# Group softmax over 285 MB: stores moved to GpSimdE's DMA queue, larger tiles, and another order at both ends

## The chip, the cores and the metric

The kernel runs on one core of a Trainium2 chip. Its data lie in the chip's memory (HBM) and pass through the core's on-chip buffer (SBUF, 128 partitions) by way of 16 DMA engines. Three compute engines matter: VectorE (DVE in the profile), ScalarE (ACT) and GpSimdE (POOL). SyncE (SP) computes nothing and issues DMAs. The engines run side by side and wait for one another on semaphores; a DMA adds 16 to its semaphore in all, one for each DMA engine that has finished its share.

The metric is the device time of one execution in microseconds (us): 1330.17 us before the change, the median of nine runs from 1329.59 to 1332.29.

## What is computed

```python
B, N, D, G = 4, 4096, 4352, 8
def reference(x):                      # x: (B, N, D) float32
    Dg = D // G                        # 544
    x_g = x.reshape(B, N, G, Dg)
    x_g = x_g - x_g.max(axis=-1, keepdims=True)
    exp = np.exp(x_g)
    out = exp / exp.sum(axis=-1, keepdims=True)
    return out.reshape(B, N, D)
```

Each of the 16,384 rows has eight groups of 544 numbers, and each group goes through a softmax of its own. Input and output are 285.2 MB each, and each is moved once: 570.4 MB.

## The kernel before

The rows are cut into 64 tiles. A tile is 256 rows of the matrix; each of the 128 partitions holds R = 2 whole rows of it, one after the other, which lie together in HBM too: 34,816 bytes. One such row on all 128 partitions (128 x 4352 elements, 2.2 MB) is the unit of computation, called a row below; there are 128 of them, numbered n, in ring slots s. The ring has NT = 5 buffers (line 50), and everything is done in place in them.

For each row there are four steps. `vector_max` (line 62) takes the maximum of the eight groups, negated, in one VectorE instruction. `scalar_exp` (line 79) lets ScalarE take the exponential of each group in turn, with the negated maximum as bias, and has it add up each group's sum on the way (eight instructions). `vector_scale` (line 68) takes the reciprocal of the eight sums and multiplies the row by it, two VectorE instructions.

The order on VectorE is written out (lines 130 to 143): the maximum of row n+1 stands before the scaling of row n, so that ScalarE has work while VectorE scales. The maximum of a tile's first row waits until the whole tile has landed (line 65), and so the scaling of a tile's last row, which stands behind it, waits for the next tile as well.

SyncE issues every DMA, both ways, on its one queue. It first loads four tiles (lines 107 and 108). After that, for each tile t, it waits until both of its rows are scaled and stores it (`store`, line 98), then waits until store t-1 has landed and loads tile t+4 into the buffer that this has freed (`step`, line 102). The loop runs twelve times over five steps, the rest is written out behind it, and at the end SyncE waits for the last five stores (lines 118 and 119). GpSimdE has nothing to do.

Of the kernel before, what the change touches and what calls it, by code (L numbers as in the profile page):

```python
# [1 line left out]

# [4 lines left out]


@with_exitstack
def kernel(  # L10
    ctx: ExitStack,
    tc: tile.TileContext,
    x: bass.AP,
    out: bass.AP,
):
    nc = tc.nc
    G = 8
    P = 128
    R = 2
    NT = 5  # L20
    S = R * NT
    AHEAD = NT - 1
    xf = x.flatten_outer_dims()
    of = out.flatten_outer_dims()
    N, D = xf.shape
    Dg = D // G
    nt = N // (P * R)
    nr = nt * R
    turns = (nr - 1) // S
    ring_turns = (nt - AHEAD) // NT  # L30
    steps = ring_turns * NT
    f32 = mybir.dt.float32
    X = mybir.AxisListType.X
    Exp = mybir.ActivationFunctionType.Exp
    xt = xf.rearrange("(t p r) d -> t p (r d)", p=P, r=R)
    ot = of.rearrange("(t p r) d -> t p (r d)", p=P, r=R)
    turn_in = xf[AHEAD * P * R:(AHEAD + steps) * P * R, :].rearrange(
        "(u b p r) d -> u b p (r d)", b=NT, p=P, r=R)
    turn_out = of[:steps * P * R, :].rearrange("(u b p r) d -> u b p (r d)", b=NT, p=P, r=R)

    landed = [tc.alloc_semaphore(f"landed{b}") for b in range(NT)]
    stored = [tc.alloc_semaphore(f"stored{b}") for b in range(NT)]

    max_done = tc.alloc_semaphore("max_done")
    exp_done = tc.alloc_semaphore("exp_done")
    rec_done = tc.alloc_semaphore("rec_done")
    scaled = tc.alloc_semaphore("scaled")

    ctx.enter_context(tc.tile_critical(no_gpsimd_drain=True))  # L49
    bufs = [ctx.enter_context(nc.sbuf_tensor(f"xt{b}", [P, R * D], f32)) for b in range(NT)]  # L50
    mx = ctx.enter_context(nc.sbuf_tensor("mx", [P, S, G], f32))
    sm = ctx.enter_context(nc.sbuf_tensor("sm", [P, S, G], f32))
    rs = ctx.enter_context(nc.sbuf_tensor("rs", [P, S, G], f32))

    def take(engine, sem, n=1):
        engine.sem_inc(sem, -n).wait_op(sem, n, "sem-ge")

    def row(s):
        b, r = divmod(s, R)
        return bufs[b][:, r * D:(r + 1) * D].rearrange("p (g d) -> p g d", g=G)  # L60

    def vector_max(s):
        i = nc.vector.reduce_max(out=mx[:, s, :], in_=row(s), axis=X, negate=True)  # L63
        if s % R == 0:
            i.wait_op(landed[s // R], 16, "sem-ge")
        i.then_inc(max_done, 1)

    def vector_scale(s):
        nc.vector.reciprocal(out=rs[:, s, :], in_=sm[:, s, :]).wait_op(  # L69
            exp_done, s + 1, "sem-ge").then_inc(rec_done, 1)  # L70
        xr = row(s)
        nc.vector.tensor_tensor(  # L72
            out=xr,
            in0=xr,
            in1=rs[:, s, :].unsqueeze(2).to_broadcast([P, G, Dg]),
            op=mybir.AluOpType.mult,
        ).wait_op(rec_done, s + 1, "sem-ge").then_inc(scaled, 1)

    def scalar_exp(s):
        xr = row(s)  # L80
        for g in range(G):
            i = nc.scalar.activation(  # L82
                out=xr[:, g, :],
                in_=xr[:, g, :],
                func=Exp,
                bias=mx[:, s, g:g + 1],
                scale=1.0,
                accum_out=sm[:, s, g:g + 1],
            )
            if g == 0:  # L90
                i.wait_op(max_done, s + 1, "sem-ge")
        i.then_inc(exp_done, 1)


    def load(t, source):
        nc.sync.dma_start(out=bufs[t % NT][:, :], in_=source).then_inc(landed[t % NT], 16)  # L96

    def store(t, target):
        take(nc.sync, scaled, R)
        nc.sync.dma_start(out=target, in_=bufs[t % NT][:, :]).then_inc(stored[t % NT], 16)  # L100

    def step(t, source, target):
        store(t, target)
        take(nc.sync, stored[(t - 1) % NT], 16)
        load(t + AHEAD, source)

    for t in range(AHEAD):
        load(t, xt[t])
    nc.sync.sem_inc(stored[NT - 1], 16)
    with nc.sync.Fori(0, ring_turns) as u:  # L110
        for t in range(NT):
            step(t, turn_in[u, t], turn_out[u, t])
    for t in range(steps, nt):
        if t + AHEAD < nt:
            step(t, xt[t + AHEAD], ot[t])
        else:
            store(t, ot[t])
    for t in range(nt - NT, nt):
        nc.sync.wait_ge(stored[t % NT], 16)

    nc.scalar.preload_act_table(Exp)  # L121
    with nc.scalar.Fori(0, turns):
        for s in range(S):
            scalar_exp(s)
        nc.scalar.sem_inc(max_done, -S)
    for n in range(turns * S, nr):
        scalar_exp(n % S)


    vector_max(0)  # L130
    with nc.vector.Fori(0, turns):
        for s in range(S):
            if s == S - 1:
                for b in range(NT):
                    nc.vector.sem_inc(landed[b], -16)
            vector_max((s + 1) % S)
            vector_scale(s)
        nc.vector.sem_inc(exp_done, -S)
        nc.vector.sem_inc(rec_done, -S)
    for n in range(turns * S, nr):  # L140
        if n + 1 < nr:
            vector_max((n + 1) % S)
        vector_scale(n % S)


# [1 line left out]
_INS = ['x']  # L147
_OUTS = [((4, 4096, 4352), 'float32')]


# [23 lines left out]
```

## Time and profile before

| | |
|---|---|
| median of nine runs | 1330.17 us |
| the profiled execution | 1331.32 us |
| its span in the profile | 1329.3 us |
| maximum of a row (VectorE, line 63), 128 times | 4681 ns |
| reciprocal of a row's sums (VectorE, line 69), 128 times | 193 ns |
| scaling of a row (VectorE, line 72), 128 times | 4692 ns |
| exponentials of a row (ScalarE, line 82, eight instructions) | 5.97 us |
| ScalarE's waiting for maxima, in all | 541.7 us |
| issue of a DMA on SyncE | 0.34 to 0.35 us |
| a load, from its issue to its landing (median of 64) | 30.6 us |
| a store, from its issue to its landing (median of 64) | 40.3 us |

The span is the part of the execution that the profile covers, and the execution is a little longer. The table's rows are durations of single instructions or transfers; whether they count depends on what they lie beside. A landing time holds the time that a transfer stands in the queue behind others, so it is no measure of how fast the transfer itself moves.

### The profile page before, as it was taken

The numbers are of one execution on the slowest core, as the hardware profiler recorded it, in microseconds if no ns is written. First come the engines' busy times: TensorE is split into PE (matmuls) and PEld (weight loads), VectorE is DVE, ScalarE is ACT, GpSimd is POOL, SyncE is SP. The second block draws the span as 40 slices with busy tenths as digits, with TensorE's granted clock in tenths as the row PEclk, the third lists the DMA queues.
The fourth block names the chain that finished last, engine by engine and source line by source line (L and its number), as shares of the span: only waits on it lengthen the run. The fifth ranks groups of instructions, "written<-read, shape, count | busy, mean of one in ns | idle before, by whom it ended". The sixth has DMA issues, their size and how long they took to land. (4 is left out here: it accounts for less than half of the span.)

```text
span 1329.3 us, 3155 instructions
## 1 busy us (share of the span) xinstructions
DVE 1207.8 (91%) x384; ACT 764.4 (58%) x2049; POOL 0.2 (0%) x4
## 2 busy tenths in 40 slices
DVE  5999999989898898998989989989899898998994
ACT  3656565655565555655556556555565555655652
POOL 0000000000000000000000000000000000000000
DMA  9999999999999999999999999999999999999997
GB/s 402 418 434 433 432 425 430 433 434 431 435 433 427 433 436 434 436 435 433 428 432 436 435 436 434 431 431 433 436 434 435 436 428 430 435 435 436 434 435 328
DMA packets 18435, 570.46 MB, mean 429 GB/s; under 512 B 2048, under 2 KB 2048, under 8 KB 2048
## 3 DMA queue, kind: packets, MB, share of 16 engines
q1 hardware_dynamic: 18432, 570.43, 99.6%
q14 instruction: 3, 0.02, 0.0%
HBM read 285.21 MB, written 285.21 MB: 429 GB/s over the span
## 5 line engine op out<-in xcount | busy, mean ns | idle before, releaser
L82 ACT ACTIVATE xt<-xt,mx 128x544 f32<-128x544 f32 x1024 | 751.3, 734 | 541.7 <-DVE mx L63 541.7
L63 DVE TENSOR_REDUCE mx<-xt 128x8 f32<-128x4352 f32 x128 | 599.1, 4681 | 97.2 <-DMA xt<-in_x_dram 97.2
L72 DVE TENSOR_TENSOR xt<-xt,rs 128x4352 f32<-128x4352 f32 x128 | 600.6, 4692 | 4.4
L82 ACT ACTIVATION_READ_ACCUMULATOR xt<-xt,mx 128x1 f32 x1024 | 191.0, 187 | 0.0
L69 DVE RECIPROCAL rs<-sm 128x8 f32<-128x8 f32 x128 | 24.7, 193 | 2.6 <-ACT xt L82 2.6
L121 ACT ACT_TABLE_LOAD x1 | 1.3, 1283 | 0.9 <-SPq L49 0.9
L158 POOL MEMSET const-bfloat16-1.0<- 128x1 bf16 x1 | 0.1, 101 | 0.0
L158 POOL MEMSET const-uint8-127<- 128x1 uint8 x1 | 0.1, 101 | 0.0
L158 POOL MEMSET const-float32-0.0<- 128x1 f32 x1 | 0.1, 98 | 0.2 <-issue 0.2
L158 POOL MEMSET const-float32-1.0<- 128x1 f32 x1 | 0.1, 98 | 0.0
## 6 DMA issues: line engine op xcount, KB each, us to landing
xt<-in_x_dram SPq DMA_DIRECT2D x64, 4352.0 KB, 30.6
out_dram<-xt SPq DMA_DIRECT2D x64, 4352.0 KB, 40.3
```

Of the source, the lines that this page charges most:

```text
L63: i = nc.vector.reduce_max(out=mx[:, s, :], in_=row(s), axis=X, negate=True)
L69: nc.vector.reciprocal(out=rs[:, s, :], in_=sm[:, s, :]).wait_op(exp_done, s + 1, "sem-ge").then_inc(rec_done, 1)
L72: nc.vector.tensor_tensor(out=xr, in0=xr, in1=rs[:, s, :].unsqueeze(2).to_broadcast([P, G, Dg]), op=mybir.AluOpType.mult,).wait_op(rec_don ...
L82: i = nc.scalar.activation(out=xr[:, g, :], in_=xr[:, g, :], func=Exp, bias=mx[:, s, g:g + 1], scale=1.0, accum_out=sm[:, s, g:g + 1],)
L121: nc.scalar.preload_act_table(Exp)
L158: nc = _bacc.Bacc("TRN2", target_bir_lowering=False, num_devices=1)
```

## The change

The ring has four buffers of three rows each (R = 3, NT = 4), so a partition's share of a tile is 52,224 bytes. There are 42 tiles of three rows and one of two.

SyncE issues all loads, written out one by one without a loop. Load t waits for store t-4 and for nothing else. The first and the last tile are loaded row by row, three and two DMAs, each row with a semaphore of its own, on which VectorE's maximum of that row waits.

GpSimdE issues the stores of tiles 0 to 40, each when its three rows are scaled. The stores of the last two tiles are issued by SyncE, behind its last load; they have their own semaphores, `last_scaled` and `last_stored`. GpSimdE waits for its last two stores and then runs a drain of its own, while SyncE's two are under way.

ScalarE's loop is built by another call, with an option that fixes where its first instruction stands; one more instruction ahead of the loop comes with it. What VectorE and ScalarE compute, and in which order, is as before.

```diff
-    R = 2
-    NT = 5
+    R = 3
+    NT = 4
...
+    sizes = nr // R * [R]
+    if nr % R:
+        sizes.append(nr % R)
+    nt = len(sizes)
     turns = (nr - 1) // S
-    ring_turns = (nt - AHEAD) // NT
+    LAST = 2
+    ring_turns = (nt - LAST) // NT
...
+    def tile_of(af, t):
+        lo = t * P * R
+        return af[lo:lo + P * sizes[t], :].rearrange("(p r) d -> p (r d)", p=P)
...
-    def vector_max(s):
+    def vector_max(n):
+        s = n % S
         i = nc.vector.reduce_max(out=mx[:, s, :], in_=row(s), axis=X, negate=True)
-        if s % R == 0:
+        r = n % R
+        if r == 0:
             i.wait_op(landed[s // R], 16, "sem-ge")
+        elif n < R:
+            i.wait_op(first_landed[r - 1], 16, "sem-ge")
+        elif n // R == nt - 1:
+            i.wait_op(last_landed[r - 1], 16, "sem-ge")
         i.then_inc(max_done, 1)
...
-        ).wait_op(rec_done, s + 1, "sem-ge").then_inc(scaled, 1)
+        ).wait_op(rec_done, s + 1, "sem-ge").then_inc(
+            scaled if n // R < nt - LAST else last_scaled, 1)
...
+    for t in range(nt):
+        if t >= NT:
+            nc.sync.wait_ge(stored[t % NT], 16 * (t // NT))
+        tile_in, source = bufs[t % NT], tile_of(xf, t)
+        if 0 < t < nt - 1:
+            nc.sync.dma_start(out=tile_in[:, :], in_=source).then_inc(landed[t % NT], 16)
+            continue
+        others = last_landed if t else first_landed
+        for r in range(sizes[t]):
+            nc.sync.dma_start(
+                out=tile_in[:, r * D:(r + 1) * D], in_=source[:, r * D:(r + 1) * D],
+            ).then_inc(others[r - 1] if r else landed[t % NT], 16)
+    rows = 0
+    for t in range(nt - LAST, nt):
+        rows += sizes[t]
+        nc.sync.wait_ge(last_scaled, rows)
+        nc.sync.dma_start(
+            out=tile_of(of, t), in_=bufs[t % NT][:, :sizes[t] * D]).then_inc(last_stored, 16)
+    nc.sync.wait_ge(last_stored, 16 * LAST)
...
     def store(t, target):
-        take(nc.sync, scaled, R)
-        nc.sync.dma_start(out=target, in_=bufs[t % NT][:, :]).then_inc(stored[t % NT], 16)
...
+        take(nc.gpsimd, scaled, R)
+        nc.gpsimd.dma_start(out=target, in_=bufs[t % NT][:, :]).then_inc(stored[t % NT], 16)
+
+    with nc.gpsimd.Fori(0, ring_turns) as u:
         for t in range(NT):
-            step(t, turn_in[u, t], turn_out[u, t])
...
+            store(t, turn_out[u, t])
+    for t in range(steps, nt - LAST):
+        store(t, tile_of(of, t))
+    for t in range(nt - NT, nt - LAST):
+        nc.gpsimd.wait_ge(stored[t % NT], 16 * (t // NT + 1))
+    nc.gpsimd.drain()
 
     nc.scalar.preload_act_table(Exp)
-    with nc.scalar.Fori(0, turns):
+    with nc.Fori(0, turns, engines=OrderedEngineSet([nc.scalar.engine]),
+                 head_slot={nc.scalar.engine: 0}):
         for s in range(S):
             scalar_exp(s)
```

## The prediction

> **What bounds the kernel now.** I read the busy rows first, then the queue table, then the loads and stores of the last third in order of time, the stretches, and last the chain of waits. From the page:
>
> ```profile
> DVE 1207.8 (91%) x384; ACT 764.4 (58%) x2049; POOL 0.2 (0%) x4
> ...
> q1 hardware_dynamic: 18432, 570.43, 99.6%
> ...
> HBM read 285.21 MB, written 285.21 MB: 429 GB/s over the span
> ```
>
> The 16 DMA engines are busy all the time; VectorE has 121 us of slack, ScalarE more. So time is bytes over rate, plus what is lost at the ends. The issues of SyncE, in order of time (start, duration):
>
> ```profile
> 1194.02 0.34 SPq L96 DMA_DIRECT2D xt<-in_x_dram  x1
> 1194.61 0.35 SPq L100 DMA_DIRECT2D out_dram<-xt  x1
> 1214.59 0.34 SPq L96 DMA_DIRECT2D xt<-in_x_dram  x1
> 1215.18 0.35 SPq L100 DMA_DIRECT2D out_dram<-xt  x1
> ```
>
> One load and one store (8.913 MB) per 20.57 us is 433.3 GB/s. Three stretches (bounds, length, busy time of DVE, ACT and POOL, clock, DMA share, GB/s):
>
> ```profile
> 350.00:1250.00 900.00, 825.48 (x262) 519.70 (x1396) 0.00 (x0) 1.00 1.00 433
> 1250.00:1310.00 60.00, 55.36 (x20) 35.78 (x96) 0.00 (x0) 1.00 0.99 429
> 1310.00:1328.00 18.00, 2.00 (x1) 0.00 (x0) 0.00 (x0) 1.00 0.67 286
> ```
>
> The middle is flat at 433; only the last 18 us fall. The chain of waits, its last pieces (start, duration, what):
>
> ```profile
> 1296.44 4.61 DVE mx L63
> 1301.05 0.02 issue
> 1301.07 5.97 ACT xt L82 x16
> 1307.04 0.02 issue
> 1307.07 0.21 DVE rs L69
> 1307.28 0.02 issue
> 1307.30 4.69 DVE xt L72
> ```
>
> It names VectorE and ScalarE for the end, but that is the chain up to the last store's issue at 1312.1. The trace also keeps every packet and every completion count, and these say more. Of 16,384 data packets of 34,816 bytes, 96% last exactly 1288 ns, an instruction fetch of 8192 bytes lasts 309 ns, and a completion count 9 ns. So a packet costs bytes / 27.2 per ns, plus 8 ns. The 16 counts of one transfer come within 0.3 us of each other in the first loads, but within 7.0 us from 333 us on: some engines have fallen behind. The last store counts from 1323.6 to 1328.0; its slowest engine still had the store before it until 1317.7, then 8 x 1.288 us. **The slowest engine never ran dry.** Its account: first packet 2.0, 1024 packets x 1.288 = 1318.9, 128 counts x 0.009 = 1.2, last count 1328.0; so 5.9 us are left over: first-packet delay (0.77 us a packet), last receipt, and stalls. The span ends 1.3 us later.
>
> **The change, part by part.**
>
> Packets. A tile of three rows makes packets of 52,224 bytes: 52,224/27.2 + 8 = 1928 ns. Row-by-row loads have 17,408 bytes, 648 ns. Per engine: 41 loads and 42 stores of three rows (664 x 1.928 = 1280.2), the last store 8 x 1.288 = 10.3, five row loads 40 x 0.648 = 25.9, 89 counts = 0.8: in all 1317.2 against 1320.1, **-2.9 us**. No row shows packets of this size or of GpSimd's queue; if larger packets saved nothing it would be 0.
>
> Stores on GpSimd. Each of the 41 issues there costs more than SyncE's 0.35 us; no row shows it. Between 0.35 and 5 us (the top is one VectorE multiply of 4.69 us, should GpSimd be held off for its length) it hides, since the previous store is still moving when the next is issued (below); I take 1 us. What is queued behind a waiting store on GpSimd is only the next store, and SyncE's loads no longer stand behind a wait for scaling. The rate is the unknown. The Trainium skill ("DMA: Bandwidth & Descriptors", Measured) gives 425 GB/s for a 16 MB transfer issued from GpSimd; the row above gives 433 for SyncE. Stores on GpSimd are 120/128 of 285.2 MB = 267.4 MB: 617.1 us at 433.3, 629.2 at 425, so +12.1 us by the page. I take the row, because it fixes the time of a packet by its bytes on the engine, whoever wrote its descriptor; no run here shows which is right.
>
> Stalls. Of the 5.9 left over, some 1.1 us is delay and receipt (first load: 2.0 + 10.3 + 1.1 = 13.4, its first count). The rest is stalls: from 40 to 335 us 127 packets ran over 1300 ns, 42 us more than normal in sum, bunched where all engines go from load to store together, and nearly none after they had drifted apart by a third of the 20.6 us round. After, loads and stores alternate packet by packet, a round of 2 x 1.93 us, so a much smaller drift should do. Bounds 1.1 and 5.9; I take the middle, 3.5: **-2.4**.
>
> Order at the ends. In both kernels VectorE does the maximum of row n+1 before it scales row n, so a store is issued only after the *next* tile has landed plus 9.6 us. Start, with shared queues at half rate each: tile 1 lands at 2.5 + 2 x 15.43 + 0.9 = 34.3 (15.43 = 8 packets of 1.928); store 0 is issued at 43.9 and moves from 46.5, when 17.8 us of loads are still queued, so the DMA does not run dry as its load queue ends (before: store 0 at 39.1, loads to 43). Store 0 lands at 78.2, load 3 at 82.9: store k lands 4.7 us before load k+3, and sharing in halves keeps that. At the end, zero at the landing of tile 41: VectorE's row takes 9.44 us (1286.92 to 1296.36 in its timeline), so store 40 goes at +9.6, store 41 at +38.1, and 42, whose scaling waits for the last exponentials, at +53.6. Left to move then: 13.0 us of store 39, 15.4 of store 40, 10.3 of load 42; less 0.9 already past the landing, they end at +37.8. Store 41 starts 1.6 us after its issue: **a gap of +1.8 us** that the slowest engine did not have before. Store 42 is queued in time behind it.
>
> At nothing: the first tile's rows wake VectorE at about 8.5 instead of 13.8, covered by loads until 64 us. The last tile's rows land at about +10 and +21, when VectorE is two rows behind (it comes to row 126 at +33); uncovered it would be one row's load, 5 us. The waits that they add hold up only the following scale. The early drain of GpSimd lies under SyncE's last stores, 26 us; bare, its nearest row is the drains at the end, 0.03 to 0.08 us, and those 26 us are all it has. The slot of ScalarE's loop lies under its 542 us of waiting. SyncE's unrolled loads wait for a store four tiles back, which lands 4.7 us before the load ahead does; were it late, the stores would have the engines to themselves.
>
> **The sum.** 2.0 + 1317.2 + 3.5 + 1.8 = 1324.5, plus 1.3 = a span of 1325.8 against 1329.3, -3.5 us. The profiled execution took 1331.3, the median 1330.17; applied to the median this is **1326.7 us**. Own range: left over 1.1 and no gap, 1322.5; 5.9 and the gap, 1329.1.
>
> **The rivals.**
>
> *Stores are served first, and the tail opens* (slower, 1336.9). The same page (Queues, rings and completion order) says that an engine takes its queues in turn, a packet at a time, and calls 9 to 17 descriptors to a packet typical. The row here shows one descriptor of 34,816 bytes per record, which would share in halves. If GpSimd's eight descriptors of an engine go as one packet, a store takes the engine for 15.4 us. Then loads lag by a tile, at the landing of tile 41 store 39 has gone, and what remains (10.3 + 15.4) cannot fill the 39.7 us until store 41 starts: a gap of 9 to 15 us, say 12, +10.2. It decides as soon as stores get clearly over half; being even is an edge, not a safe place. Against it: equal packet sizes.
>
> *GpSimd's stores move at the page's 425 GB/s* (slower, 1326.7 + 12.1 = 1338.8). Against: 1288 ns packets that know only bytes. If the toll at each change from load to store never faded (42 us over 16 engines and 14 rounds is 0.18 us, and there would be 340 rounds), it would be some 60 us; the fading at 333 us speaks against it.
>
> *Nothing shows* (1330): packets as long per byte as before, stalls as before, the gap offset by the tidier start.
>
> **How the numbers follow.** A measurement of this kernel tells about 0.2% from no change, 2.7 us. Forecast 0.48, stores first 0.23, slow stores or a lasting toll 0.15, nothing shows 0.14. The forecast's own range is mostly below 1327.5, partly within; so faster 0.45, same 0.16, slower 0.39. The range runs from 1322 to 1337.5: it holds the forecast, no change, and most of the first rival.
>
> **What would show it.** Right: store packets of 52,224 bytes at 1928 ns; a flat DMA rate of about 434 with both queues busy; store 41 issued some 38 us after tile 41's landing and a hole of under 3 us; the last counts within 3 us of each other. Wrong: loads that take longer to land than stores and a hole of 10 us near the end (first rival); store packets in pieces or longer (second); a middle below 431 GB/s.

## The result, and the profile after

The changed kernel takes 1336.19 us (median of ten runs, 1331.29 to 1343.13) beside 1330.39 us for the kernel before: 1.0048 times the time, 95% interval 1.0036 to 1.0060. It is slower, where faster was forecast. The runs also spread over 12 us, those of the kernel before over 4. Ratios here leave out runs over 1.5% above the fastest of their kernel, so with a wide spread a ratio is lower than the median suggests.

The page of the changed kernel (busy rows, queues, then groups and issues; columns as before):

```profile
DVE 1206.8 (90%) x384; ACT 764.4 (57%) x2049; POOL 22.1 (2%) x45
...
q1 hardware_dynamic: 6912, 296.36, 51.7%
q0 software_dynamic: 5904, 274.07, 47.5%
...
L137 POOL DMA_DIRECT2D out_dram<-xt x41 | 21.9, 534 | 1256.7 <-POOLq L66 1256.7
...
xt<-in_x_dram SPq DMA_DIRECT2D x41, 6528.0 KB, 39.0
out_dram<-xt POOLq DMA_DIRECT2D x41, 6528.0 KB, 43.2
```

There are two data queues now and the compute engines work as long as before. An issue on GpSimdE takes 534 ns. Where the time went is in the stretches (last two columns: DMA share, GB/s):

```profile
42.00:100.00 58.00, 57.80 (x19) 37.19 (x102) 1.20 (x2) 1.00 0.99 388
100.00:350.00 250.00, 224.11 (x73) 140.95 (x380) 4.25 (x8) 1.00 1.00 433
350.00:1250.00 900.00, 826.42 (x263) 523.30 (x1406) 15.93 (x30) 1.00 1.00 434
1250.00:1310.00 60.00, 57.37 (x19) 35.79 (x96) 0.53 (x1) 1.00 0.88 377
```

The kernel before, first of these stretches:

```profile
42.00:100.00 58.00, 57.80 (x20) 35.78 (x96) 0.00 (x0) 1.00 0.99 422
```

The middle is as good as before. From 42 to 100 us, when the first stores meet the queued loads, the rate falls to 388 with the engines busy (0.99): packets run long there. From 1250 to 1310 us it falls to 377 because engines are idle (0.88). As a sum, I call *lost* the length of a stretch less its bytes at 434 GB/s, from the packet records, so it is a mean over the 16 DMA engines:

| lost, us | before | after |
|---|---|---|
| 2 to 42 us | 1.1 | 1.1 |
| 42 to 100 us | 1.2 | 5.6 |
| 100 to 350 us | 1.7 | 1.0 |
| 350 to 1250 us | 1.6 | 0.4 |
| 1250 us to the last packet | 5.5 | 8.7 |
| sum | 11.2 | 16.8 |

The difference, 5.6 us, is that of the spans (1334.9 and 1329.3).

A mean does not say which engine sets the end. The records carry no engine number, but in the busy stretches a packet starts about 3 ns before the record of the one ahead of it ends, so they can be strung into 16 sequences. *An engine's loss* is here the time from 2.0 us on less its packets and counts at the prediction's prices (1928 ns for 52,224 bytes). By 1235 us the slowest engine has lost 11.7 us in the changed kernel, 10.2 of them by 120 us, and the median engine 4.3. In the kernel before, the slowest has lost 5.8, and 4.0 by 120 us.

The chain of waits of the changed kernel, at the point where it turns from DMAs to VectorE (start, duration, what):

```profile
1186.30 43.14 DMA out_dram<-xt
1229.44 0.02 issue
1229.45 38.98 DMA xt<-in_x_dram
1268.43 0.02 issue
1268.45 4.69 DVE mx L74
```

The store of tile 37 frees the buffer, tile 41 is loaded into it and lands at 1268.4, and from there VectorE's chain waits only once, 1.2 us for ScalarE, near its end. Its timeline, from that landing to the last scaling:

```profile
1268.45 4.69 DVE L74 TENSOR_REDUCE mx<-xt 128x8 f32<-128x4352 f32 x1 [2.42 <-DMA xt<-in_x_dram]
...
1306.19 4.68 DVE L74 TENSOR_REDUCE mx<-xt 128x8 f32<-128x4352 f32 x1
...
1317.13 4.69 DVE L89 TENSOR_TENSOR xt<-xt,rs 128x4352 f32<-128x4352 f32 x1
```

The last store is issued at 1321.9 and lands at 1333.6, 65.2 us after tile 41. Of the 16 counts of tile 41 fourteen come from 1262.1 to 1264.6, the last two at 1268.0 and 1268.4. The time between the first and the last count of a transfer is called *drift* below; in the last row's load it is 23 us (1282.1 to 1305.2). Before the store of tile 41, the slowest engine is idle for 2.2 us and the next for 3.2, the other fourteen for 7.3 to 10.2: they wait for the slow ones.

### The profile page after: what moved, and what is told of

Read it like the earlier page. It is cut to its first block, busy times and chain, and to the rows that moved or that the text cites. A ratio compares the mean times of both kernels' runs of the same rounds, so it can differ in the third digit from the quotient of the medians.

```text
span 1334.9 us, 2846 instructions
## 1 busy us (share of the span) xinstructions
DVE 1206.8 (90%) x384; ACT 764.4 (57%) x2049; POOL 22.1 (2%) x45
## 3 DMA queue, kind: packets, MB, share of 16 engines
q0 software_dynamic: 5904, 274.07, 47.5%
## 5 line engine op out<-in xcount | busy, mean ns | idle before, releaser
L137 POOL DMA_DIRECT2D out_dram<-xt x41 | 21.9, 534 | 1256.7 <-POOLq L66 1256.7
## 6 DMA issues: line engine op xcount, KB each, us to landing
out_dram<-xt SPq DMA_DIRECT2D x1, 6528.0 KB, 16.8
out_dram<-xt SPq DMA_DIRECT2D x1, 4352.0 KB, 11.7
```

The costliest lines, as they stand in the source:

```text
L137: nc.gpsimd.dma_start(out=target, in_=bufs[t % NT][:, :]).then_inc(stored[t % NT], 16)
```

## The experiments

All changes are against the changed kernel unless said otherwise; ratios are against the kernel before. "Mean stall" is what the packets of a stretch lasted beyond bytes / 27.2 + 8 ns, divided by the 16 engines; a packet that lasts longer than that is *stalled*.

**One queue.** Tiles, buffers and row-by-row ends stay; SyncE issues everything, three tiles ahead.

```diff
+    for t in range(nt):
+        take(nc.sync, scaled, R); nc.sync.dma_start(...)       # store t
...
+            nc.sync.wait_ge(stored[(t - 1) % NT], 16 * ((t - 1) // NT + 1))
+            load(t + AHEAD)
```

> The changed kernel with its three-row tiles and row-by-row ends, but all loads and stores on SyncE's one queue again, in the order of the kernel before (three tiles ahead). Theory A (two queues that alternate packet by packet cost some 6 us around 42 to 100 us, and let the loads lag so that VectorE's chain ends late): both go, the larger packets stay worth 2.9 us, so 1326 to 1329. Theory B (the tile size and four buffers make the end late): stays at 1334 or more.

Measured: 1329.01 us, 0.9989 (0.9981 to 0.9997). Stretches:

```profile
42.00:100.00 58.00, 57.80 (x19) 37.19 (x101) 0.00 (x0) 1.00 0.99 419
350.00:1250.00 900.00, 825.35 (x263) 522.08 (x1402) 0.00 (x0) 1.00 1.00 434
1250.00:1310.00 60.00, 55.47 (x20) 35.78 (x96) 0.00 (x0) 1.00 0.95 410
```

The dip to 388 is gone, and tile 41 lands at 1259.5 instead of 1268.4. Three-row tiles are no cause by themselves; with one queue they win a little. The edit also loads three tiles ahead instead of four, so alone it does not part the second queue from the deeper order.

**Two rows, five buffers, two queues.**

```diff
-    R = 3
-    NT = 4
+    R = 2
+    NT = 5
```

> The changed kernel with two rows to a tile and five buffers, all else as changed (stores on GpSimdE, the last two on SyncE). Theory A: the toll at the start stays, packets cost as before, one row less of VectorE's chain at the end: 1333 to 1338, slower than before. Theory B (tile size): back to about 1330.

Measured: 1330.70 us, 1.0001 (0.9993 to 1.0009). Hardly a stall and little drift (2.9 us in the middle): from 42 to 100 us the mean stall is below 0.1 us and 0.1 us is lost, so theory A as I had it, that alternating queues cost time as such, is wrong.

**Last tiles stored row by row.**

```diff
-        rows += sizes[t]
-        nc.sync.wait_ge(last_scaled, rows)
-        nc.sync.dma_start(out=tile_of(of, t), ...)
+        for r in range(sizes[t]):
+            rows += 1
+            nc.sync.wait_ge(last_scaled, rows)
+            nc.sync.dma_start(out=tile_of(of, t)[:, r * D:(r + 1) * D], ...)
```

> The changed kernel, but the last two tiles are stored row by row on SyncE, each row as soon as it is scaled. If the end is set by VectorE's chain after the landing of the last full tile (53.8 us) and then a whole tile's store (11.4 us): the last transfer is half as long and the hole is filled, so 2.5 to 4.6 us less than the changed kernel, about 1332.5. If the slowest DMA engine sets the end by its bytes: 1336, no change.

Measured: 1335.63 us, 1.0036 (1.0020 to 1.0051), runs from 1328.5 to 1349.0. In the traced execution the end came 63.1 us after tile 41's landing instead of 65.2, but tile 41 landed at 1271.3. The spread hides a gain of 2 us; this settles nothing by its time.

**A head start for half the engines.**

```diff
+    nc.sync.dma_start(out=tile_of(of, nt - 2)[0:16:2, :], in_=tile_of(xf, 0)[0:16:2, :]).then_inc(skewed, 16)
     for t in range(nt):
```

> The changed kernel with one extra small DMA ahead of all loads: eight pieces of 52,224 bytes, one for each of eight DMA engines, copied from the input to a place in the output that is written over later. It puts these engines one packet (1.93 us) behind the others. If the stalls between 42 and 100 us come from all 16 engines changing direction together, they mostly go: 1330 to 1333, mean stall per engine there under 3 us instead of 5.4. If they come from two queues as such, the time is 1336 to 1338.

Measured: 1343.78 us, 1.0055 (1.0037 to 1.0073), runs from 1334.4 to 1356.7. Mean stall from 42 to 100 us 5.1 us against 5.4, and from 350 to 1250 us 6.2 us are lost (0.4 in the changed kernel). That all engines change direction together is not the reason: with half of them a packet behind, they stall as much.

**Short packets both ways.** Eight unused numbers after each row in the buffer.

```diff
-    bufs = [... [P, R * D] ...]
+    bufs = [... [P, R, D + 8] ...]
```

> The changed kernel with 8 unused numbers between a partition's rows in the buffer, so that loads and stores move in packets of 17,408 bytes (648 ns) instead of 52,224; tiles, buffers, queues and order as changed. By the packet rate alone this costs 8 ns on each of 1365 more packets per engine, 10.9 us. If the stalls of the changed kernel come from long packets that alternate on an engine: they go (mean stall per engine from 42 to 100 us under 1.5 us), and the time is 1334 to 1340 with a narrow spread. If they come from three-row tiles or four buffers as such: stalls and spread stay, 1344 to 1350.

Measured: 1332.81 us, 1.0025 (1.0015 to 1.0035), runs from 1332.5 to 1334.7. Mean stall from 42 to 100 us 0.8 us. Though each engine has 1365 packets more, it is faster than the changed kernel, and steady.

**Stores on ScalarE's queue**, run twice.

```diff
-        nc.gpsimd.dma_start(out=target, ...)
+        nc.scalar.dma_start(out=target, ...)     # behind the exponentials of the next row
```

> The changed kernel with the 41 stores issued by ScalarE on its own hardware queue instead of GpSimdE, each behind the exponentials of the row after the tile, when its last scaling is over. If GpSimdE's queue causes the stalls: mean stall from 42 to 100 us under 2 us, 1327 to 1331. If it is two queues with packets of 52,224 bytes, whoever issues them: like the changed kernel, 1333 to 1340, with its wide spread.

> The kernel with stores on ScalarE's queue once more, for a second trace: its times fell in two groups, 1327 to 1331 and 1337 to 1340, and its first trace is of the slow group. If the groups differ by how far the DMA engines have drifted apart: in a fast execution the first and the last count of a transfer lie under 9 us apart in the middle (17.8 in the slow one), and tile 41 lands on its last engine 8 to 10 us earlier, before 1263. If they differ by the bytes' rate: the same spread of the counts, and longer packets in the slow one.

Measured: 1.0027 (1.0010 to 1.0043); the 22 runs lie from 1327.5 to 1331.2 or from 1337.5 to 1340.3. The first trace (1338.7 us), then the second (1332.6 us):

```profile
350.00:1250.00 900.00, 819.99 (x262) 518.56 (x1392) 0.00 (x0) 1.00 1.00 433
1250.00:1310.00 60.00, 57.37 (x19) 36.11 (x98) 0.00 (x0) 1.00 0.77 334
```

```profile
350.00:1250.00 900.00, 819.82 (x262) 518.49 (x1393) 0.00 (x0) 1.00 1.00 433
1250.00:1310.00 60.00, 57.39 (x19) 36.69 (x99) 0.00 (x0) 1.00 0.87 376
```

Up to 1250 us the two move the same bytes, and their mean stalls are the same (3.7 and 3.6 us up to there). What differs is how the stalls fall on the engines. In the first trace one engine has lost 14.1 us by 1235 us and no other more than 3.3; in the second the slowest has lost 7.9, no other more than 3.8. So the drift in the middle (median) is 17.8 us in the first and 5.7 in the second, tile 41 lands at 1270.4 or 1264.3, and the last packet ends at 1335.2 or 1329.1: 6.1 us apart, beside 6.2 us in the slowest engine's loss. That engine is last with its loads and with its stores: at 1235 us it is some seven packets behind. A transfer has landed only when its last engine has counted, so slow packets on one engine cost the whole kernel their time, and the mean does not show them. The slow packets of the first trace's engine come all along: 8.3 us by 120 us, 14.1 by 1235.

No trace shows one of the fastest runs, with a landing before 1263. With GpSimdE out of the matter the spread stays, and so does one slow engine: neither its queue nor its drain, nor the fixed place of ScalarE's first instruction, which this edit leaves out too, is needed for it. Whether GpSimdE's queue adds to it is open, as the intervals overlap.

**Two rows, row-by-row last stores, five and six buffers.** The second and third experiments together, and one buffer more for the other.

```diff
-    R = 3
-    NT = 4
+    R = 2
+    NT = 5          # the other: 6
...
+        for r in range(sizes[t]):
+            rows += 1
+            nc.sync.wait_ge(last_scaled, rows)
...
```

> Two rows to a tile and five buffers (the earlier variation), and the last two tiles stored row by row. In that variation all engines were idle some 6 us near the end and ended together with the last store of 10.3 us of data. If VectorE's chain and then the last transfer set the end there: half a transfer less, 5 us, so 1325 to 1327, faster than the kernel before. If the engines' bytes do: 1330.

> As the one with two rows and row-by-row last stores, but six buffers, the same buffer bytes as in the changed kernel. If the number of buffers matters (loads lag because the ring of buffers has no slack): 1 to 2 us less than with five. If not: the same within 0.5 us. If it is the buffers' bytes that bring the stalls: a spread of over 5 us and stalls as in the changed kernel.

Measured: 1328.37 and 1328.42 us, both 0.9993 (0.9985 to 1.0001). The first is 2.3 us below the kernel with whole tiles (1330.70), but the kernel before was 0.7 us quicker beside it too (1329.67 and 1330.34), so some 1.6 us are left, a third of what was expected, and the intervals of the ratios overlap. In the traces the last count comes at 1324.9 instead of 1327.4, and its 16 counts lie 3.7 us apart instead of 0.2: the slowest engine then ends alone. A sixth buffer brings nothing.

**Row by row one way.** Stores, then loads, in 17,408-byte packets, the other way in 52,224.

```diff
-        nc.gpsimd.dma_start(out=target, in_=bufs[t % NT][:, :])...
+        for r in range(R):
+            take(nc.gpsimd, scaled)
+            nc.gpsimd.dma_start(out=target[:, r * D:(r + 1) * D], ...)
```

> The changed kernel with GpSimdE's stores row by row (17,408-byte packets, each row when it is scaled); loads stay whole tiles of 52,224-byte packets. The packets alone cost 5 us more per engine. If an engine takes its two queues in turn by packets, loads get three quarters of it, tile 41 lands early (by 1258, against 1268 in the changed kernel), no hole is left at the end, 1328 to 1331. If long load packets beside a second queue are what stalls: stalls from 42 to 100 us stay at 4 us or more and the time is 1334 or more.

> The opposite: all loads row by row (17,408-byte packets; VectorE still waits for the whole tile), stores whole tiles of 52,224-byte packets. If the queues are taken in turn by packets, stores get three quarters, loads lag, tile 41 lands at 1268 or later although no packet stalls, engines are idle 12 us or more near the end, 1336 to 1341. If the share doesn't follow the packets' size: like the one with small packets both ways, 1328 to 1333.

Measured: 1365.53 us, 1.0261 (1.0217 to 1.0305), and 1377.85 us, 1.0370 (1.0354 to 1.0385), far from what either theory put. Engines do take their queues in turn, packet by packet, whatever its size: with row-by-row stores the packet records of an engine read load, store, load, store, 1928 and 648 ns, until the loads have run out, and then stores alone. But a share of three quarters helps neither way: the queue that is ahead runs out of work, I infer because the buffers that it needs next are held by the other. The second, in the middle:

```profile
350.00:1250.00 900.00, 797.49 (x255) 502.88 (x1349) 14.88 (x28) 1.00 1.00 421
```

421 GB/s is 26.7 us lost in this stretch (22.0 in the other), most of it load packets that run over their length (a mean stall of 17.3 us, 17.9 in the other), the short ones here, the long ones there. Why unequal packets stall is open.

**One queue and row-by-row last stores.** The first experiment's order, with the third's edit to its last two stores.

```diff
+            for r in range(sizes[t]):
+                rows += 1
+                nc.sync.wait_ge(last_scaled, rows)
+                nc.sync.dma_start(out=tile_of(of, t)[:, r * D:(r + 1) * D], ...)
```

> Three-row tiles on SyncE's one queue (the first experiment), with the last two tiles stored row by row. There the last engine was busy to within 2 us of the end and the others idle for 5, so half a transfer less at the end brings 1 to 2 us: 1327 to 1328. If VectorE's chain alone sets the end: 5 us, 1324.

Measured: 1328.53 us, 0.9992 (0.9983 to 1.0000). Half a microsecond above what was expected, and no better than two rows on two queues.

**Two rows, four buffers.**

```diff
-    R = 3
+    R = 2
     NT = 4
```

> The changed kernel with two rows to a tile and four buffers (139 KB a partition instead of 209). With two rows and five or six buffers nothing stalled. If the packet's length decides: still no stalls (mean under 1.5 us from 42 to 100 us), the counts within 6 us, 1330 to 1333. If four buffers, that is a ring without slack, bring the drift: counts 8 us or more apart in the middle, and a spread of the times of over 5 us.

Measured: 1336.40 us, 1.0044 (1.0030 to 1.0058), runs from 1336.1 to 1336.8. With two rows and two queues, first five buffers, then four:

```profile
1250.00:1310.00 60.00, 55.10 (x18) 35.04 (x95) 1.06 (x2) 1.00 0.99 428
```

```profile
1250.00:1310.00 60.00, 56.46 (x19) 35.71 (x97) 1.06 (x2) 1.00 0.92 398
```

One buffer less costs 5.7 us, at the end, with small stalls (mean 1.8 us from 42 to 100 us) and the counts 2.1 us apart in the middle (6.0 at the last full tile). Both of my theories said otherwise: short packets do not save a ring of four, and the loss needs no large drift. The slowest engine has lost only 3.2 us by 1235 us, but is itself idle for 6.6 us after that, 2.8 with five buffers. The last full tile lands at 1276.8 on its last engine, against 1269.0. So a short ring costs time here in another way than in the changed kernel, whose slowest engine is idle for 2.7 us.

**A late first store.**

```diff
+    nc.gpsimd.wait_ge(scaled, R + 2)
     with nc.gpsimd.Fori(0, ring_turns) as u:
```

> The changed kernel with the first store held back until two rows of the second tile are scaled (about 64 us instead of 45), when the first four tiles have been loaded; so the two queues do not alternate while the seven first loads run. A hole of up to 3 us opens at 64 us. If the stalls belong to the meeting with the piled-up loads: mean stall from 42 to 100 us under 2 us (5.4 in the changed kernel), 1328 to 1333. If long packets stall wherever both queues are full: they come later instead, 1334 to 1340.

Measured: 1.0073 (1.0059 to 1.0087): one run at 1333.5, five from 1339.7 to 1340.7. The trace is of the first. Mean stall from 42 to 100 us 1.5 us, as expected if the stalls belong to the meeting with the seven loads. In the trace 2.5 us are lost from 42 to 100 us, and 8.4 from 1250 us on, about as in the changed kernel. Again the mean misleads: the slowest engine has still lost 6.2 us by 120 us and 8.9 by 1235 (11.7 in the changed kernel), and this execution is 3.1 us shorter than the traced one of the changed kernel. Why the other five take 1340 us no trace shows; over all runs the late store brings no gain.

The losses side by side, from the traces (the runs vary, so one execution each). The first two columns of losses are means; then come the slowest engine's loss by 1235 us and its idle time after that:

| | queues | buffers x rows | lost 42 to 100 | lost from 1250 on | slowest engine lost | slowest engine idle | last full tile lands | last count |
|---|---|---|---|---|---|---|---|---|
| before | 1 | 5 x 2 | 1.2 | 5.5 | 5.8 | 0 | 1286.9 (the last of all) | 1328.0 |
| changed | 2 | 4 x 3 | 5.6 | 8.7 | 11.7 | 2.7 | 1268.4 | 1333.6 |
| one queue | 1 | 4 x 3 | 1.2 | 5.4 | 6.3 | 0 | 1259.5 | 1326.3 |
| two rows | 2 | 5 x 2 | 0.1 | 6.5 | 1.9 | 2.8 | 1269.0 | 1327.4 |
| two rows, four | 2 | 4 x 2 | 2.0 | 9.9 | 3.2 | 6.6 | 1276.8 | 1332.5 |
| ScalarE, slow | 2 | 4 x 3 | 1.7 | 14.4 | 14.1 | 2.0 | 1270.4 | 1335.6 |
| ScalarE, faster | 2 | 4 x 3 | 1.3 | 8.4 | 7.9 | 1.6 | 1264.3 | 1329.4 |
| late first store | 2 | 4 x 3 | 2.5 | 8.4 | 8.9 | 1.8 | 1265.3 | 1330.4 |

In the four traces with two queues and four buffers of three rows, the last count less the slowest engine's loss is 1321.5 to 1321.9 us: they differ by that loss and by nearly nothing else.

## Why the prediction was wrong

*Packets: right in length, too high in worth.* Nine in ten and more of the 52,224-byte packets last 1928 ns, on both queues, and the middle runs at 434. But on a busy engine the next packet starts 3 ns before the record ends: from start to start 1924.7 ns, 1284.7 for 34,816 bytes and 644.7 for 17,408. Priced so, the saving is 1.8 us, not 2.9 (and every engine's loss above is about 2 us more with three rows, 3 us with two). The one-queue kernel took 1.3 us less than the kernel before; from 100 to 1250 us the changed kernel lost 1.9 us less.

*Stores on GpSimdE: right.* 0.53 us an issue, hidden; its packets (1928 and, with two rows, 1288 ns) are those of SyncE. The 425 GB/s of the Trainium skill ("DMA: Bandwidth & Descriptors", Measured), a figure for loads, does not hold for these stores, and with it the rival of slow stores goes; its 12.1 us should have been 12.4, as the page shows 274.07 MB on GpSimdE's queue (123 rows of 128, not 120). The early drain took 3.4 us, from 1304.1, below SyncE's stores.

*Stalls: the step that failed.* The sum is that of the slowest engine, and it left this engine 3.5 us for stalls, first-packet delay and last receipt, because "a much smaller drift should do". In the traced execution the engine had lost 11.7 us by 1235 us. The rest of the sum holds: 2.0 + 1317.2 + 11.7, and 2.7 us idle, make 1333.6, and the last count came at 1333.6. I had read the fading of the stalls in the kernel before as a matter of engines in step. The head start for half the engines showed that it is not, and so does ScalarE's slow trace, where the engine most out of step went on losing time. Short packets, two-row tiles, one queue or a later first store each take most of the mean stall away. What makes a packet run long, and why so many fall on one engine, is open.

*Order at the ends: right for the slowest engine but for the landing of tile 41.* Of what follows that landing each date was right: stores 40, 41 and 42 issued at +10.2, +37.9 and +53.4 (predicted +9.6, +38.1, +53.6), and the slowest engine's gap before store 41 was 2.2 us (predicted 1.8). The landing itself was put at 1259.0 (1324.5 less 53.6, 1.6 and 10.3) and came at 1268.4, 9.4 us late. About 8 us of that are the slowest engine's loss (11.7 instead of 3.5). The rest fits "sharing in halves keeps that", which did not hold either: load k+3 landed 8.1 us after store k through the middle, not 4.7. The 8.7 us lost from 1250 us on, 3.2 more than before, are a mean: fourteen engines that wait for two.

*The rival on the other side* gave 1336.9 and a late tile 41, and the time came there, but not for its reason: that is luck. Stores do not take the engine for a whole tile: they alternate with loads one by one, and store 39, which should have been gone at the landing of tile 41, landed at 1283.4. What remains shown is coarser. Two queues on a ring of four buffers lose 8.4 to 14.4 us from 1250 us on, with three-row or two-row tiles, in every trace with packets of equal length over 17,408 bytes and the last two tiles stored whole; one queue on four buffers, or two queues on five, lose 5.4 to 6.5. With three rows it is mostly waiting for the slowest engine, with two rows on four buffers that engine waits too.

*At nothing: right, with one remark.* The row-by-row load of the last tile brings nothing where it is, and with two queues it can hurt, since short packets get less of an engine: with two rows and five buffers the last row landed at 1300.0, and VectorE waited for it.

The best versions here, 1328.4 and 1328.5 us, are below the kernel before by less than their intervals can tell.

## What to carry to other kernels

Where the DMA engines are full, a second queue has no rate to give (433 GB/s in the middle before, 434 after); what it changes is when transfers *complete*, and completion is the last of 16 engines. Before splitting loads and stores over queues, count the buffers that the longer completion needs, and keep the packets of both queues equally long. Predict such an end from the slowest engine, and size its stalls from a trace of the same queues and packets: a mean over 16 engines hid the cause here. Look at the spread of the runs too: it grew from 4 to 12 us. That it is the spread of the slowest engine's loss fits the four traces; the runs without a trace do not show it.

## What was not expected of the hardware

A packet's record lasts 8 ns and its bytes at 27.2 per ns, from 8192 to 52,224 bytes, in load and store, on all three issuing engines' queues: 309, 648, 1288 and 1928 ns; from start to start it is 3 ns less. Two queues with packets of 17,408 and 52,224 bytes are much worse than two with either length (22.0 to 26.7 us lost from 350 to 1250 us, against 4.6 and 0.4). And one engine of 16 can lose 14.1 us by slow packets where no other loses more than 3.3, with the mean stall of the quicker trace: on ScalarE's queue the same program took 1338.7 us so, and 1332.6 us with a slowest loss of 7.9.
